# Storing the down factors of a transformer's FFN as one plain fp32 tile instead of a hi and lo pair, and splitting them where they are used

## The chip, the core and the metric

The kernel runs on one core of one Trainium2 chip. The metric is the device time of one execution in microseconds. TensorE (PE in the profile) multiplies matrices, VectorE (DVE) and GpSimd (POOL) do elementwise work, ScalarE (ACT) does activations and copies and also issues the stores spoken of here, and SyncE (SP) issues the loads. PEld is the weight load of TensorE. SBUF is the memory on the core, PSUM the small memory that TensorE writes its products to; DRAM is off the core.

## What is computed

Two transformer blocks over 1024 tokens of width 1024, all in fp32. Each ends in a gated FFN of hidden width 2816, and that is where the change lies:

```python
gu = jnp.einsum('bsd,df->bsf', x, w_gu)
gate, up = gu[..., :FFN_HIDDEN], gu[..., FFN_HIDDEN:]
ffn = jnp.einsum('bsf,fd->bsd', jax.nn.silu(gate) * up, w_down)
...
f = (jax.nn.silu(h @ w_gate[l]) * (h @ w_up[l])) @ w_down[l]
```

## The kernel before

**Three products for one.** TensorE takes fp32r operands, a form of fp32 with a shortened mantissa. To keep fp32's precision the helper `split` (L78) turns an operand into two tiles: `hi` is a copy on ScalarE (L80), `lo` the rest, a subtract on VectorE or GpSimd (L84). `mm3` (L97 to L99) then multiplies hi by hi, hi by lo and lo by hi. So each line of matmuls in the FFN stands three times in a trace.

**Seven products for eight.** Both matrix products of the FFN use a scheme of the Strassen kind. A matrix is cut in 2 x 2 blocks; sums of blocks of the one side (`A11`, `S3`, `S2`, `A22`, `S1`, `A12`, `S4`) meet sums of the other side (`B11`, `T3`, `T2`, `T4`, `T1`, `B21`, `B22`), seven products numbered 1, 7, 6, 4, 5, 2, 3.

**The gate and up stage** (`gate_up`) walks over pairs of 128-wide slices of the hidden width: 11 pairs, the first two of them computed directly. For each later pair it makes the seven products of the gate weights and the seven of the up weights (`product`). A product takes its weight block, or a sum `tt` of two (L925), splits it into a tile `wst` (ACT copy L945, subtract L946 on DVE or POOL), and runs 12 matmuls into a PSUM bank; `after` (L958 to L976) adds the banks up into tiles called `p`, `u` and so on, and `out` (L983 to L994) applies silu and multiplies gate by up. What comes out are the four blocks of the hidden activation, tiles of 128 x 512.

**The store.** `forms` (L1034) is a generator that the loop steps once per product. It makes the sums `S1` to `S4` in place (L1055 to L1064) and calls `store` for each of the seven blocks or sums: 63 calls for nine pairs and 8 plain ones for the last four slices, 71 per FFN. `store` takes a tile `hf`, splits the block into it, and keeps the pair (destination, tile); the DMA is issued by the next call, in `flush`, on ACT's queue (L1023). Tiles `hf` and `wst`, and `ws` of the next stage, come from one ring of six, `slot("w")`: a `wst` can be written only when the tile six places earlier is free, and an `hf` is free only when its store has landed. The blocks themselves live in a ring of twelve, `post`.

**The down stage** (`down`) has five groups, of one slice pair and four times two. A group is the seven products in the order above. For each, 512 KB per slice pair are loaded to a tile `hs` of a ring of seven (the activations' tiles, free by then; in the trace they bear the activations' names, x1B11h and so on), hi and lo side by side; the `down` weights and their sums `st` (L1169) are split into `ws`; 24 matmuls of 128 x 512 follow, and VectorE adds the PSUM banks into accumulators (L1196). `T3`'s sums are POOL's only work there. The last four slices are done directly in `down_last`.

```python
        def store(self, dst, x):

            self.flush()
            t = slot("w", [P, 2, 512], F32R, "hf")
            with soon():
                split(t[:, 0], t[:, 1], x)
            self.stores.append((dst, t.bitcast(F32)))
```

**What sets the order.** The program is compiled by a list scheduler that simulates the engines; `soon()` puts a block ahead of other work that is ready. Each engine runs its instructions strictly in the order that comes out, and so does each queue of DMA issues.

Of the kernel before, what the change touches and what calls it, by code (L numbers as in the profile page):

```python
# [9 lines left out]
F32 = mybir.dt.float32  # L10
F32R = mybir.dt.float32r
# [10 lines left out]
S = 1024  # L22
D = 1024
P = 128
# [14 lines left out]
def two_blocks(ctx: ExitStack, tc: tile.TileContext, a):  # L39
# [16 lines left out]
    def slot(tag, shape, dtype, name):  # L56
        return strm.tile(shape, dtype, tag=tag, bufs=SLOTS[tag], name=name)
# [16 lines left out]
    def soon():  # L74
        return tc.high_priority(offset=4000)
# [132 lines left out]
    for h, l, k0, nk in wu0:  # L208
        for j in range(nk):
            k = k0 + j  # L210
# [566 lines left out]
    class SAct:  # L777
# [4 lines left out]
        def __init__(self, name):  # L782
            self.name = name
            self.high, self.high_done = pool(f"{name}b")
            hi = [self.high.tile([P, 4, 512], F32R, name=f"{name}{n}")
                  for n in ("B11h", "B11l", "B21h", "B21l", "B12l", "B22h", "B22l")]
            self.t = {"B11": hi[0:2], "B21": hi[2:4], "B22": hi[5:7]}

            self.ring, self.n = hi, 0

# [6 lines left out]

        def next(self):
            self.n += 1
            return self.ring[(self.n - 1) % len(self.ring)]  # L800

# [100 lines left out]
    FORMS = ("A11", "S3", "S2", "A22", "S1", "A12", "S4")  # L902
    h_d = [{n: dr.tile([P, 2, 512], F32, name=f"h_d{i}{n}") for n in FORMS} for i in range(NPAIR)]
    hl_d = [dr.tile([P, 2, S], F32, name=f"hl_d{i}") for i in range(NLAST)]

# [90 lines left out]
    class Ffn:  # L996
# [29 lines left out]
        def store(self, dst, x):  # L1026

            self.flush()
            t = slot("w", [P, 2, 512], F32R, "hf")
            with soon():  # L1030
                split(t[:, 0], t[:, 1], x)
            self.stores.append((dst, t.bitcast(F32)))

        def forms(self, i, b):  # L1034


            if i >= NPAIR:
                plain = lambda j, th: self.store(hl_d[2 * (i - NPAIR) + j][:, :, th * 512:(th + 1) * 512], b[j, th])
                for n in ((0, 0), None, (1, 1), (1, 0), None, (0, 1)):
                    if n:  # L1040
                        plain(*n)
                    yield
                return
# [85 lines left out]
        def down(self, wd, res=None):  # L1129
# [24 lines left out]
            for g, np_ in enumerate(SIZES):  # L1154
# [19 lines left out]
                for m, (p, ln, rn) in enumerate(((1, "A11", "B11"), (7, "S3", "T3"), (6, "S2", "T2"), (4, "A22", "T4"),  # L1174
                                                 (5, "S1", "T1"), (2, "A12", "B21"), (3, "S4", "B22"))):
                    hs, ws = act.next(), []
                    for j in range(np_):
                        DMA.dma_start(hs.bitcast(F32)[:, 2 * j:2 * j + 2, :], h_d[f + j][ln])
                        w = slot("w", [P, 2, 512], F32R, "ws")
                        with soon():  # L1180
                            split(w[:, 0], w[:, 1], block(rn, j))
                        ws.append(w)
# [3 lines left out]
                    for c0, n in ((0, 2), (2, 2)) if p in (1, 6, 5, 3) else ((c, 1) for c in range(4)):  # L1186
                        o = a[c0 // 2] if n == 2 else b[c0][:, None, :]
                        for i in range(n):
                            ts = slice((c0 + i) * P, (c0 + i + 1) * P)
                            for j in range(np_):  # L1190
                                mm3(o[:, i, :], hs[:, 2 * j, ts], hs[:, 2 * j + 1, ts], ws[j][:, 0], ws[j][:, 1],
                                    not more and j == 0, j == np_ - 1, more)
# [21 lines left out]
            for n in range(NLAST):  # L1214
                t = act.next()
                DMA.dma_start(flat(t).bitcast(F32), hl_d[n].rearrange("p a b -> p (a b)"))
                self.hs.append(halves(t))
            for n in range(NLAST):
                t = halves(act.next()) if n else [slot("w", [P, S], F32R, "last") for _ in range(2)]
                split(*t, nxt[n])  # L1220
                self.ws.append(t)
# [551 lines left out]
```

## Time and profile before

| | |
|---|---|
| median of 3 runs | 2727.97 us (2725.17 to 2728.15) |
| the profiled execution | 2729.37 us, span on the core 2727.6 us |
| busy | PE 89%, PEld 73%, DVE 67%, ACT 40%, POOL 29% |
| mean granted clock of TensorE | 0.945 |
| DMA | 414.00 MB, mean 152 GB/s |
| gate and up of the first FFN | about 720 to 1227 us |
| down of the first FFN | 1227 to about 1390 us |
| gate and up, down of the second FFN | about 2050 to 2503, 2503 to 2657 us |

A busy PE need not be at its peak: a matmul counts as long as it is in the pipe, at either clock. So the idle time of PE is read stage by stage, with the waits that end it, and the pace of matmuls in a stage without waits serves as measure for the others.

### The profile page before, as it was taken

Reading aid. Unit: us, or ns where it says so; the run is one execution under the profiler, and the core shown is the slowest. Engines: PE = TensorE matmul, PEld = TensorE weight load, DVE = VectorE, ACT = ScalarE, POOL = GpSimd, SP = SyncE. Lnnn points to the kernel's source line nnn. Section 1 sums busy time; section 2 is a strip of 40 time slices with the busy share of each in tenths; the row PEclk is TensorE's granted clock in tenths of the full one; section 3 lists DMA queues with packets and bytes.
Section 4 is the critical chain, followed back from the end, with each engine's and each line's share of the span. In section 5 each row is a group of like instructions: output and inputs, shape, how many; then the busy total and the mean of one; then the engine's idle time right before and its main releaser. Section 6 shows DMA issues by size and latency. Waiting matters only on the chain.

```text
span 2727.6 us, 32854 instructions
## 1 busy us (share of the span) xinstructions
PE 2419.6 (89%) x11584; PEld 1977.9 (73%) x11584; DVE 1840.7 (67%) x3042; ACT 1099.3 (40%) x2013; POOL 784.8 (29%) x751
## 2 busy tenths in 40 slices
PE   8889997998988887889997989898888898999998
PEld 8868775886766665668876868677666666777886
DVE  4889789457667777758776366767555656556775
ACT  4559864243233222323226344445733323334221
POOL 2510235037422122120026042527552212122004
PEclk9999997999998998999998999999989999899999
DMA  4153546333435554567732434553414323337763
GB/s 175 59 153 113 147 137 178 83 98 105 162 127 190 178 179 158 179 249 252 261 141 108 129 105 132 175 159 100 164 58 151 139 108 125 114 124 254 252 226 124
DMA packets 171724, 414.00 MB, mean 152 GB/s; under 512 B 21788, under 2 KB 67868, under 8 KB 170536
## 3 DMA queue, kind: packets, MB, share of 16 engines
q1 hardware_dynamic: 149064, 337.45, 38.2%
q10 hardware_dynamic: 22496, 74.46, 6.8%
q8 instruction: 92, 1.51, 0.2%
q14 instruction: 72, 0.59, 0.1%
HBM read 278.65 MB, written 133.19 MB: 151 GB/s over the span
## 4 chain that ended last, share of the span: by engine, by line
PE 51%; DVE 10%; DMA 5%; POOL 4%; issue 3%; ACT 3%; SPq 0%; ACTq 0%; DVEq 0%; POOLq 0%
PE plg L97 8%; PE plg L98 7%; PE plg L99 7%; PE pmm L97 6%; PE pmm L98 5%; PE pmm L99 5%; PE ptr L99 2%; PE ptr L97 2%; PE ptr L98 2%; DMA raw_c<-in_w_cond_dram 1%; DVE hf L84 1%; DVE wst L946 1%; DVE tt L925 1%; PE plg L337 1%; DVE mod L1278 1%
## 5 line engine op out<-in xcount | busy, mean ns | idle before, releaser
L946 POOL TENSOR_TENSOR wst<-rw,wst 128x512 fp32r<-128x512 f32 x57 | 90.0, 1578 | 406.6 <-ACT wst L945 323.9
L84 POOL TENSOR_TENSOR wl<-raw,wh 128x1024 fp32r<-128x1024 f32 (+2 forms) x28 | 66.1, 2367 | 306.4 <-ACT wh L80 280.1
L337 PE MATMUL plg<-qk,qk 128*128 128x384 f32 (+4 forms) x480 | 127.3, 383 | 29.0 <-DVE mn L350 15.7
L946 DVE TENSOR_TENSOR wst<-tt,wst 128x512 fp32r<-128x512 f32 x144 | 118.5, 826 | 23.7 <-ACT wst L945 23.6
L945 ACT CAST wst<-tt 128x512 fp32r<-128x512 f32 x144 | 88.6, 618 | 73.4 <-PE plg L99 21.4
L1574 DVE TENSOR_TENSOR_SCAN sab<-sab 128x640 f32<-128x640 f32 (+7 forms) x64 | 99.9, 1566 | 20.7 <-ACT sab L1572 19.9
L278 ACT ACTIVATE junk_a<-xi,cand 128x1024 bf16<-128x1024 f32 (+1 forms) x124 | 109.0, 879 | 12.0 <-DVE cand L267 6.9
L337 PEld LDWEIGHTS plg<-qk,qk 128*128 128x128 f32 x480 | 83.7, 202 | 39.6 <-DVE mn L350 17.7
L1196 DVE TENSOR_TENSOR dacc<-dacc,plg 128x1024 f32<-128x1024 f32 x48 | 58.5, 1220 | 55.8 <-PE plg L99 55.8
L80 ACT CAST ws<-st 128x512 fp32r<-128x512 f32 x72 | 44.9, 628 | 127.2 <-PE plg L99 86.8
L162 PE MATMUL pmm<-wh,xh 128*128 128x256 f32 (+1 forms) x320 | 92.2, 289 | 1.7 <-DVE stgl L399 0.8
L163 PE MATMUL pmm<-wl,xh 128*128 128x256 f32 (+1 forms) x320 | 91.5, 286 | 0.0
L164 PE MATMUL pmm<-wh,xl 128*128 128x256 f32 (+1 forms) x320 | 91.4, 286 | 0.0
L351 ACT ACTIVATE e<-e,mn 128x128 f32<-128x128 f32 (+7 forms) x96 | 74.1, 773 | 35.5 <-DVE mn L350 34.5
L994 POOL TENSOR_TENSOR u<-u,u 128x512 f32<-128x512 f32 x36 | 48.2, 1338 | 139.3 <-DVE u L968 113.5
L80 ACT CAST wh<-raw 128x1024 fp32r<-128x1024 f32 x54 | 56.5, 1048 | 69.0 <-PE pmm L98 29.1
L97 PE MATMUL pmm<-xh,wh 128*128 128x512 f32 x192 | 79.2, 412 | 5.8 <-DVE oB L585 3.2
L692 PE MATMUL pmm<-woh,mixh 128*128 128x512 f32 x192 | 78.9, 411 | 5.1 <-ACT mixh L681 2.7
L98 PE MATMUL pmm<-xl,wh 128*128 128x512 f32 x192 | 77.3, 403 | 0.0
L99 PE MATMUL pmm<-xh,wl 128*128 128x512 f32 x192 | 77.2, 402 | 0.0
L693 PE MATMUL pmm<-wol,mixh 128*128 128x512 f32 x192 | 76.3, 397 | 0.0
L694 PE MATMUL pmm<-woh,mixl 128*128 128x512 f32 x192 | 75.8, 399 | 0.3 <-DVE mixl L84 0.3
(733 smaller groups left out, 8361.1 us busy)
## 6 DMA issues: line engine op xcount, KB each, us to landing
raw_c<-in_w_cond_dram SPq DMA_DIRECT2D x48, 512.0 KB, 4.7
qk<-qkd SPq DMA_DIRECT2D x72, 256.0 KB, 5.7
rw<-in_wgu_dram SPq DMA_DIRECT2D x36, 512.0 KB, 3.5
rw<-in_w_down_dram SPq DMA_DIRECT2D x26, 512.0 KB, 5.2
x_d<-acc SPq DMA_DIRECT2D x24, 512.0 KB, 2.6
qk<-qk2d SPq DMA_DIRECT2D x48, 256.0 KB, 4.6
raw<-in_wqk_dram SPq DMA_DIRECT2D x20, 512.0 KB, 4.1
raw<-in_w_down_dram SPq DMA_DIRECT2D x18, 512.0 KB, 5.2
```

What stands on the lines that cost most here:

```text
L80: A.copy(hi, src)
L84: eng.tensor_tensor(lo, src, hi.bitcast(F32), op=OP.subtract)
L97: T.matmul(out, lh, rh, start=start, stop=False, skip_group_check=more)
L98: T.matmul(out, lh, rl, start=False, stop=False, skip_group_check=more)
L99: T.matmul(out, ll, rh, start=False, stop=stop, skip_group_check=more)
L162: T.matmul(o, at(0, k, tb * P, P), h[:, j, :], start=(k == 0), stop=False)
L163: T.matmul(o, at(0, k, tb * P, P), l[:, j, :], start=False, stop=False)
L164: T.matmul(o, at(1, k, tb * P, P), h[:, j, :], start=False, stop=(k == KT - 1))
L278: A.activation(junk_a[:, :L], xi[self.blks[i]], AF.Sign, bias=c, accum_out=self.cnt[:, i:i + 1])
L337: T.matmul(pl[:, c, :n], q[:, isl], k2[:, c * n:(c + 1) * n], start=(j == 0), stop=last)
L946: (G if p in (2, 4) else V).tensor_tensor(wl, x, wh.bitcast(F32), op=OP.subtract)
L1574: V.tensor_tensor_scan(sa[:, ::-1], sa[:, ::-1], sa[:, ::-1], 1.0, op0=OP.mult, op1=OP.bypass)
```

## The change

`store` no longer splits. It keeps the block's own tile, which goes to DRAM as 128 x 512 fp32, 256 KB instead of 512 KB. In `down` the plain blocks are loaded into four half tiles cut from two of the seven tiles of the ring (`next_raw`), and split from there into the other five (`next`), hi on ACT and lo on POOL for products 1, 2, 4 and 3, on DVE for 7, 6 and 5. The subtract of the `ws` of product 3 moves from DVE to POOL. The last four slices are split before `down_last`, with lo on POOL, and the tiles of their weights are drawn from other places.

```diff
-            self.ring, self.n = hi, 0
+            self.ring, self.n, self.m = hi, 0, 0
...
         def next(self):
+
             self.n += 1
-            return self.ring[(self.n - 1) % len(self.ring)]
+            return self.ring[2 + (self.n - 1) % 5]
+
+        def next_raw(self):
+
+            self.m += 1
+            k = (self.m - 1) % 4
+            return self.ring[k // 2].bitcast(F32)[:, k % 2 * 2:k % 2 * 2 + 2, :]
...
-    h_d = [{n: dr.tile([P, 2, 512], F32, name=f"h_d{i}{n}") for n in FORMS} for i in range(NPAIR)]
-    hl_d = [dr.tile([P, 2, S], F32, name=f"hl_d{i}") for i in range(NLAST)]
+    h_d = [{n: dr.tile([P, 512], F32, name=f"h_d{i}{n}") for n in FORMS} for i in range(NPAIR)]
+    hl_d = [dr.tile([P, S], F32, name=f"hl_d{i}") for i in range(NLAST)]
...
             self.flush()
-            t = slot("w", [P, 2, 512], F32R, "hf")
-            with soon():
-                split(t[:, 0], t[:, 1], x)
-            self.stores.append((dst, t.bitcast(F32)))
+            self.stores.append((dst, x))
...
-                plain = lambda j, th: self.store(hl_d[2 * (i - NPAIR) + j][:, :, th * 512:(th + 1) * 512], b[j, th])
+                plain = lambda j, th: self.store(hl_d[2 * (i - NPAIR) + j][:, th * 512:(th + 1) * 512], b[j, th])
...
-                    hs, ws = act.next(), []
+                    hr = act.next_raw()[:, :np_, :]
                     for j in range(np_):
-                        DMA.dma_start(hs.bitcast(F32)[:, 2 * j:2 * j + 2, :], h_d[f + j][ln])
+                        DMA.dma_start(hr[:, j, :], h_d[f + j][ln])
+                    hs = act.next()
+                    hh, hl = hs[:, 0:np_, :], hs[:, 2:2 + np_, :]
+                    ws = []
+                    with soon():
+                        split(hh, hl, hr, lo_eng="pool" if p in (1, 2, 4, 3) else "dve")
+                    for j in range(np_):
                         w = slot("w", [P, 2, 512], F32R, "ws")
                         with soon():
-                            split(w[:, 0], w[:, 1], block(rn, j))
+                            split(w[:, 0], w[:, 1], block(rn, j), lo_eng="pool" if p == 3 else "dve")
                         ws.append(w)
...
-                                mm3(o[:, i, :], hs[:, 2 * j, ts], hs[:, 2 * j + 1, ts], ws[j][:, 0], ws[j][:, 1],
+                                mm3(o[:, i, :], hh[:, j, ts], hl[:, j, ts], ws[j][:, 0], ws[j][:, 1],
                                     not more and j == 0, j == np_ - 1, more)
...
-                t = act.next()
-                DMA.dma_start(flat(t).bitcast(F32), hl_d[n].rearrange("p a b -> p (a b)"))
-                self.hs.append(halves(t))
+                r = flat(act.next_raw())
+                DMA.dma_start(r, hl_d[n])
+                self.hs.append(halves(act.next()))
+                split(*self.hs[n], r, lo_eng="pool")
             for n in range(NLAST):
-                t = halves(act.next()) if n else [slot("w", [P, S], F32R, "last") for _ in range(2)]
+                t = [slot("w", [P, S], F32R, "last") for _ in range(2)] if n < 2 else halves(act.ring[0] if n == 2 else act.next())
                 split(*t, nxt[n])
```

The change moves instructions, since the scheduler places them anew. Three places matter. In the orders below the names of tiles are those of the text above; line numbers after the change lie 7 to 10 higher (L945 is L952, L1023 is L1030, L1169 is L1173).

First, ScalarE in the gate and up stage of the first FFN, around the first stores of the fifth pair (`h_d4`). Before:

```order
L985 ACTIVATE p_8084<-p_8084 128x512
L80 CAST hf<-s_8132 128x512
L945 CAST wst<-rw 128x512
L945 CAST wst<-tt 128x512
L1023 DMA h_d4A_6142<-hf 128x1024
L985 ACTIVATE u_8111<-u_8111 128x512
L80 CAST hf<-u_8168 128x512
L945 CAST wst<-rw 128x512
L1023 DMA h_d4A_6145<-hf 128x1024
L80 CAST hf<-p_8084 128x512
L945 CAST wst<-tt 128x512
L945 CAST wst<-rw 128x512
```

The same stretch of ScalarE's queue with the change:

```order
L992 ACTIVATE p_8015<-p_8015 128x512
L952 CAST wst<-tt 128x512
L1030 DMA h_d4A_6142<-s_8060 128x512
L952 CAST wst<-rw 128x512
L992 ACTIVATE u_8039<-u_8039 128x512
L952 CAST wst<-tt 128x512
L965 COPY p_8336<-pmm 128x512
L952 CAST wst<-tt 128x512
L1030 DMA h_d4A_6145<-u_8093 128x512
L952 CAST wst<-rw 128x512
L952 CAST wst<-tt 128x512
L1030 DMA h_d4A_6147<-p_8015 128x512
```

The copies `hf` are gone from between the copies `wst`; the issues of the stores stay in ScalarE's queue, and each now waits for the block itself, made by POOL or DVE.

Second, POOL in the down stage of the first FFN, from its last multiply of the stage before. Before, these are all its instructions of the rest of that stage:

```order
L994 TENSOR_TENSOR u_10123<-u_10123,u_10261 128x512
L1169 TENSOR_TENSOR st<-rw 128x512
L1169 TENSOR_TENSOR st<-raw,rw 128x512
L1169 TENSOR_TENSOR st<-raw 128x512
L1169 TENSOR_TENSOR st<-rw 128x512 x2
L1169 TENSOR_TENSOR st<-raw 128x512
```

With the change, one group of two slice pairs out of the middle of that stage:

```order
L1173 TENSOR_TENSOR st<-raw 128x512
L1173 TENSOR_TENSOR st<-rw 128x512
L84 TENSOR_TENSOR x1B12l<-x1B11h,x1B12l 128x1024
L84 TENSOR_TENSOR x1B21h<-x1B11h,x1B21h 128x1024
L84 TENSOR_TENSOR x1B22l<-x1B11l,x1B22l 128x1024
L84 TENSOR_TENSOR ws<-rw,ws 128x512
L84 TENSOR_TENSOR x1B21l<-x1B11h,x1B21l 128x1024
L84 TENSOR_TENSOR ws<-raw,ws 128x512
L1173 TENSOR_TENSOR st<-rw 128x512
```

POOL goes from two subtracts per group to eight, four of them 128 x 1024 wide.

Third, TensorE in the first group of two slice pairs of that stage, in product 7 (`S3` by `T3`; its four banks are two `pmm` and two `ptr`, its two slices have one `ws` each). Before, on the first bank `ptr`:

```order
L97 MATMUL ptr_10601<-ws_10588,x1B11l_6107 128x512
L98 MATMUL ptr_10601<-ws_10588,x1B11l_6107 128x512
L99 MATMUL ptr_10601<-ws_10588,x1B11l_6107 128x512
L97 MATMUL ptr_10601<-ws_10594,x1B11l_6107 128x512
L98 MATMUL ptr_10601<-ws_10594,x1B11l_6107 128x512
L99 MATMUL ptr_10601<-ws_10594,x1B11l_6107 128x512
```

With the change, where `x1B22h` holds the same factor and `plg` is a product of the group before:

```order
L98 MATMUL ptr_10406<-ws_10394,x1B22h_6111 128x512
L99 MATMUL ptr_10406<-ws_10394,x1B22h_6111 128x512
L97 MATMUL ptr_10406<-ws_10399,x1B22h_6111 128x512
L98 MATMUL ptr_10407<-ws_10394,x1B22h_6111 128x512
L99 MATMUL ptr_10407<-ws_10394,x1B22h_6111 128x512
L97 MATMUL ptr_10407<-ws_10399,x1B22h_6111 128x512
L97 MATMUL plg_10181<-ws_10335,x1B21l_6109 128x512
```

On the banks `ptr` the second slice's L98 and L99, which need lo tiles, no longer follow its L97, which needs hi tiles alone, and another product is put between; on `pmm` they stood apart before, too.

## Rows read from the trace of the kernel before

**Rows 1.** Windows, three stages: us, busy (x count) of PE, PEld, DVE, ACT, POOL, PEclk, DMA, GB/s.

```profile
720.00:1227.00 507.00, 424.98 (x1673) 325.44 (x1671) 353.20 (x460) 154.59 (x273) 108.10 (x70) 0.93 0.52 182
1227.00:1390.00 163.00, 162.87 (x691) 131.88 (x692) 125.29 (x170) 43.85 (x69) 8.67 (x6) 0.99 0.68 243
...
2050.00:2503.00 453.00, 402.05 (x1603) 309.75 (x1601) 269.23 (x376) 146.71 (x260) 95.77 (x71) 0.95 0.38 139
```

**Rows 2.** Waits of PE, 720 to 1227 us: releaser, us in total, times, longest.

```profile
PE plg L97 <- ACT wst L945: 14.4, 5, 5.0
PE pmm L97 <- ACT wst L945: 13.5, 4, 6.6
PE plg L97 <- DVE u L966: 11.8, 7, 3.4
PE plg L97 <- DVE u L968: 11.4, 10, 3.7
PE pmm L1295 <- ACT mh L80: 9.5, 5, 4.3
PE plg L99 <- DVE wst L946: 8.2, 7, 1.8
```

**Rows 3.** Waits of PE, 2050 to 2503 us.

```profile
PE pmm L97 <- ACT wst L945: 12.1, 7, 3.1
PE plg L97 <- ACT wst L945: 12.0, 7, 1.7
PE plg L97 <- DVE u L968: 8.1, 10, 0.9
PE plg L99 <- DVE wst L946: 4.7, 7, 0.7
PE plg L97 <- ACT ws L80: 3.6, 1, 3.6
```

**Rows 4.** Timeline around one such wait: start, us, engine, line, [idle before it <- releaser].

```profile
2271.17 0.33 ACTq L1023 DMA_DIRECT2D h_d5S<-hf  x1
2271.54 0.62 ACT L945 CAST wst<-raw 128x512 fp32r<-128x512 f32 x1 [0.58 <-DVE hf L84]
...
2272.21 0.79 PE L97 MATMUL pmm<-x3B11h,wst 128*128 128x512 f32 x1 [3.14 <-ACT wst L945]
```

**Rows 5.** Windows, the 2.8 us behind that wait.

```profile
2272.20:2275.00 2.80, 2.79 (x7) 2.21 (x8) 2.09 (x5) 0.77 (x2) 0.00 (x0) 0.50 0.73 294
```

**Rows 6.** Windows, instructions on the tile hf alone: us, DVE and ACT busy (x count).

```profile
720.00:1227.00 507.00, 49.22 (x71) 43.94 (x71) 0.93 0.52 182
```

**Rows 7.** Chain of waits, 720 to 1227 us, its sum by line.

```profile
by line: PE plg L97 11.2%; PE plg L98 10.2%; PE plg L99 10.1%; PE pmm L97 6.0%; PE pmm L98 5.8%; DMA raw_c<-in_w_cond_dram 5.7%; PE pmm L99 5.7%; issue 4.3%; PE ptr L99 3.3%; PE ptr L97 3.2%; PE ptr L98 3.2%; DVE mod L1278 3.2%; DVE hf L84 
```

**Rows 8.** Windows, one group of two slice pairs in the first down stage.

```profile
1252.00:1290.50 38.50, 38.50 (x167) 31.18 (x166) 30.83 (x42) 8.69 (x14) 2.94 (x2) 1.00 0.67 240
```

**Rows 9.** The page, groups: count, then busy us, mean ns, then idle before.

```profile
L84 POOL TENSOR_TENSOR wl<-raw,wh 128x1024 fp32r<-128x1024 f32 (+2 forms) x28 | 66.1, 2367 | 306.4 <-ACT wh L80 280.1
...
L80 ACT CAST wh<-raw 128x1024 fp32r<-128x1024 f32 x54 | 56.5, 1048 | 69.0 <-PE pmm L98 29.1
```

**Rows 10.** Line L84, 0 to 300 us: ns min/median/max, first and last start, form.

```profile
L84 DVE TENSOR_TENSOR wl<-raw,wh x2: 1226/1226/1227, 35.9 to 37.4; 128x1024 fp32r<-128x1024 f32 x2
```

**Rows 11.** Timeline of POOL and of DVE, 1316 to 1319 us.

```profile
1316.86 1.29 POOL L1169 TENSOR_TENSOR st<-rw 128x512 f32<-128x512 f32 x1 [31.61 <-DMA rw<-in_w_down_dram]
...
1316.93 1.76 DVE L84 TENSOR_TENSOR ws<-raw,ws 128x512 fp32r<-128x512 f32 x1
1318.62 0.68 DVE L84 TENSOR_TENSOR ws<-rw,ws 128x512 fp32r<-128x512 f32 x1
```

**Rows 12.** Line L1196, 1227 to 1390 us: ns min/median/max.

```profile
L1196 DVE TENSOR_TENSOR dacc<-dacc,plg x22: 1208/1221/1221, 1256.3 to 1383.5; 128x1024 f32<-128x1024 f32 x22
```

**Rows 13.** Groups of DVE by shape, 1252 to 1290.5 us.

```profile
L84 DVE TENSOR_TENSOR ws<-st,ws 128x512 fp32r<-128x512 f32 x8 | 6.4, 819 | 0.0
```

**Rows 14.** DMA on the tile hf, whole span.

```profile
DMA to landing us min/median/max: 2.6/2.7/8.5
```

## The prediction, written before the changed kernel was run

> **What bounds the kernel now.** I read the windows by stage first, since a busy share over the whole span mixes stages with different limits. In the first down stage PE is busy 162.87 of 163 us: nothing but TensorE's pace counts there, one matmul of 128 x 512 per 163/691 = 0.236 us. In the gate and up stages it is not so: PE is busy 425 of 507 us and 402 of 453, so 82 + 51 = 133 us are idle [rows 1]. At the pace of down, their 1673 and 1603 matmuls would take 395 and 378 us, and the stages are 112 and 75 us longer than that, 187 in all. So behind each idle microsecond stand 0.41 us more in which PE works, but slowly. The reason can be seen behind one stall: after 3.14 us of idleness the next 2.8 us have a granted clock of 0.50, the 1.2 GHz level, and matmuls follow each other at half the pace [rows 4, 5]. I count each idle microsecond of PE as 1.41 us of time.
>
> Next, who ends PE's waits. In the first gate and up stage 27.9 us end with the hi copy of a `wst` on ACT and 8.2 with its lo half on DVE, 36.1 together; 23.2 us end with VectorE reading a PSUM bank (L966, L968); 9.5 with a step of the conditioning rows that are woven into this stage (L1295) [rows 2]. In the second, 24.1 + 4.7 = 28.8 us are for `wst`, 8.1 for L968, and 3.6 for the first `ws` of down [rows 3]. ACT itself is only 30% busy [rows 1], so its copies are late because they wait. The timeline shows how: the issue of a store stands in ACT's queue until DVE has made the lo half of `hf`; the `wst` copy right behind it starts when it is through, and PE has by then been idle for 3.14 us [rows 4]. Besides, each `hf` holds a place of the ring that `wst` needs until its store has landed, 2.6 to 8.5 us after its issue [rows 14].
>
> **What is removed.** In the first gate and up stage 71 splits, 43.9 us of ACT and 49.2 us of DVE [rows 6], and by the code as many in the second. ACT has room, so its share alone is worth nothing; what counts is the queue and the ring. All six places of the ring now go to `wst`, so a weight can be split up to six products ahead, and the order of ACT shows the copies next to each other. For the second stage I take nine tenths of the 28.8 us: 25.9. The first has the same cause, but DVE is 353 of 507 us busy there, and still would be 304 of a shorter stage; also, 5.7% of its chain of waits are loads of the conditioning rows and 3.2% the steps on them [rows 7], which the change leaves. So I take half of 36.1: 18.0. Of the waits for L966 and L968, those of the second stage are 0.8 us each (8.1 by 10), a round trip over PSUM that stays. In the first stage 17 of them come to 23.2 us, of which 17 x 0.8 = 13.6 are that trip; the other 9.6 are a late DVE, and I let them go with its 49 us. Sum of idle time removed: 25.9 + 18.0 + 9.6 = 53.5, times 1.41: **75 us**. The wait of 3.6 us at the start of down [rows 3] goes too, as the last stores hold no place that `ws` needs; counted for both FFNs, 2 x 3.6 x 1.41 = **10 us**. Gain: 85 us. Its ends: nothing if waits only change their name; and if all waits for `wst`, L966 and L968 went, (36.1 + 28.8 + 23.2 + 8.1) x 1.41 + 10 = 146 us.
>
> **What is added, in down.** Take a group of two slice pairs, 38.5 us, in which PE is full, DVE busy 30.8, ACT 8.7, POOL 2.9 [rows 8]. ACT gets seven copies of 128 x 1024 at 1.05 us [rows 9], 7.3 us: it has the room. DVE gets three subtracts of that width at 1.23 [rows 10], 3.7 us, and loses two of 0.68 [rows 11]: 33.1 us, still under 38.5. POOL gets four wide subtracts at 2.37 [rows 9] and two narrow ones at 1.29 [rows 11], 12.1 us, for 15 of 38.5. Each fits by itself. But POOL and DVE disturb each other: a `ws` subtract that began 0.07 us behind a POOL subtract of 1.29 us took 1.76 instead of 0.68 us, so it stood still for 1.08 of the 1.29 [rows 11]. Adding a PSUM bank into an accumulator was never slowed, 1.22 us at most [rows 12]. What DVE loses to POOL's 12.1 us is not in the trace; it lies between nothing and all of it. Before, eight `ws` subtracts of one group were (0.82 - 0.68) x 8 = 1.1 us late [rows 13] to POOL's 2.9. I take half, 6.0, since the new POOL subtracts start where DVE's `ws` subtracts start, at the end of a product. DVE then has 39.1 us of work for 38.5: 0.6 us too much, in eight such groups 5 us. At the start of each down stage the order of PE puts another product between the hi and lo matmuls of product 7, so lo tiles are late there; I price that with the wait found at this place before, 3.6 us [rows 3], twice: 7. Loss: 12 x 1.41 = **17 us**; ends 0 and, with the whole 12.1 lost, (45.2 - 38.5) x 8 = 54, plus 7, times 1.41: 86.
>
> **The rest** costs nothing. Stores and loads are halved; DMA is 68% busy in down [rows 1] and PE waits for no load there. The number of DMA issues on ACT and SP stays. The ring of `hs` falls from seven products to five of 5.7 us (24 x 0.236), far more than a load and a split need. A block must now outlive its store before `post` can reuse it; what is late then is the next product's first tile, a rival below.
>
> **Sum.** The profiled execution took 2729.4 us, 1.4 more than the median of the runs. 2729.4 - 85 + 17 = 2661.4 there, against the median **2660 us**.
>
> **Rivals.** *POOL chokes DVE in down.* If DVE loses all 12.1 us, a group needs 45.2; and DVE cannot fill each gap, since it waits for PE's results too. If half of the 7.7 us that it idles now remain, a group takes 49.0, 10.5 more: 8 x 10.5 + 7 = 91, times 1.41 = 129 us lost against 85 gained, **2772 us**. It decides from (85/1.41 - 7)/8 = 6.7 us per group on. For it: the 1.08 us of standstill [rows 11] and the place of the new subtracts. Against it: POOL's work is spread over the group and accumulation is not touched [rows 12]. The Trainium skill ("SBUF — State Buffer", section "Who interferes with whom") says that a VectorE instruction with two inputs in SBUF and a GpSimd one that reads SBUF exclude each other for a whole instruction, whichever begins first. The 1.76 and the untouched 1.22 us agree with it; by that rule alone every new subtract of POOL can cost DVE its full length, which is this rival.
>
> *The conditioning rows hold the first stage.* If they, and not `wst`, set its pace, the 18.0 and 9.6 us stay: 25.9 x 1.41 + 10 - 17 = 30 us gained, **2698 us**. For it: the 9.5 us of waits for L1295 [rows 2] and the 5.7% [rows 7].
>
> *The waits move to the post ring.* If blocks held by stores delay the next product as `hf` did, only the 9.6 us go: 14 - 17, **2731 us**, no change. For it: stores that land after up to 8.5 us [rows 14]; against it, twelve places instead of six, most stores land in 2.7 us, and each is half as long.
>
> **How the numbers follow.** Forecast 0.67, conditioning rows 0.15, post ring 0.06, choked DVE 0.12. Some 0.2% (5.5 us) is what a measurement of this kernel can tell from no change. Forecast and conditioning rows are both faster: 0.82; the post ring is the same: 0.06; the choke is slower: 0.12. The forecast's own spread goes from all waits gone with the loss of 17 left (2729.4 - 146 + 17 - 1.4 = 2599) to a third of its gain (28 - 17, 2717); the conditioning rows lie inside. So 2600 to 2716; the other two are left out with 0.18.
>
> **What would show it.** Right: no L80 on `hf`; PE idle in the gate and up stages down from 133 to about 75 us, with waits for `wst` a third of what they were; in down, POOL near 15 and DVE near 39 us per group, PE still full but for about 1 us. Wrong: groups of 42 us or more with PE waiting for lo tiles; waits of ACT or DVE for stores of `h_d` before `p` and `u` tiles; or an unchanged first stage with longer waits for L1295.

## The result, and the profile after

The changed kernel takes 2576.26 us in the median of four runs (2570.38 to 2576.77), the kernel before 2728.06 in four runs beside it: a ratio of 0.9433, 95% interval 0.9407 to 0.9459. 152 us are gone; the forecast was 68 (2660 us, 2600 to 2716). The direction was right, the time lies below the range. The profiled execution took 2576.43 us.

The windows of the changed kernel, in the order gate and up of the first and of the second FFN, down of the first and of the second. Columns as in [rows 1].

```profile
720.00:1127.00 407.00, 391.98 (x1658) 310.53 (x1658) 313.73 (x388) 121.07 (x206) 112.07 (x68) 1.00 0.52 171
1962.00:2330.00 368.00, 363.12 (x1548) 290.86 (x1547) 215.83 (x299) 112.04 (x191) 99.41 (x68) 1.00 0.30 103
1127.00:1304.00 177.00, 171.78 (x724) 137.00 (x723) 161.01 (x179) 72.17 (x102) 77.15 (x39) 0.98 0.45 142
2330.00:2503.00 173.00, 169.14 (x733) 136.95 (x732) 158.91 (x167) 80.22 (x117) 77.28 (x39) 1.00 0.46 143
```

In gate and up PE was idle 82 and 51 us [rows 1]; now it is idle 407 - 391.98 = 15 and 368 - 363.12 = 5. The granted clock of these stages rose from 0.93 and 0.95 to 1.00: with the stalls, the running at the lower level behind them [rows 5] went too. DVE is 314 of 407 us busy in the first stage, a higher share than before, and PE is full all the same. The waits of PE that are left, first stage, with engine, line, releaser, us in total, times and longest:

```profile
PE ptr L99 <- DVE wst L953: 4.0, 2, 2.0
PE pmm L97 <- ACT wst L952: 2.8, 2, 2.1
PE plg L97 <- DVE u L973: 2.2, 2, 1.5
PE pmm L99 <- DVE wst L953: 1.6, 1, 1.6
PE pmm L1306 <- ACT mh L80: 1.0, 1, 1.0
PE ptr L97 <- ACT wst L952: 1.0, 2, 0.7
PE plg L97 <- DVE u L975: 0.9, 1, 0.9
PE plg L97 <- ACT wst L952: 0.7, 1, 0.7
```

The lines are 7 to 11 higher than before (L945 is L952, L966 and L968 are L973 and L975, L1295 is L1306, L1196 is L1206). Set against [rows 2]: ACT's `wst`, 27.9 us, is 2.8 + 1.0 + 0.7 = 4.5 now; the 23.2 us for the PSUM readers L966 and L968 are 3.1; the 9.5 us of the conditioning rows are 1.0. In the second stage hardly anything is left of [rows 3]:

```profile
PE ptr L99 <- DVE wst L953: 2.0, 1, 2.0
PE pmm L97 <- ACT wst L952: 1.9, 4, 0.5
PE ptr L97 <- ACT wst L952: 0.7, 1, 0.7
PE plg L97 <- DVE p L978: 0.3, 1, 0.3
```

What ACT waits for tells more than its busy time does. The kernel before, 720 to 1227 us:

```profile
ACT hf L80 <- POOL u L994: 52.6, 11, 6.6
ACT s L983 <- PE pmm L99: 48.9, 9, 6.9
ACT p L985 <- DVE p L971: 35.5, 7, 5.7
ACT u L985 <- DVE u L976: 32.1, 9, 4.7
ACT hf L80 <- POOL p L994: 22.5, 9, 3.5
ACT hf L80 <- DVE s L992: 22.0, 9, 3.5
```

The changed kernel, 720 to 1140 us:

```profile
ACT wst L952 <- PE plg L99: 98.5, 48, 4.8
ACT p L965 <- PE pmm L99: 21.6, 11, 3.4
ACT wst L952 <- PE ptr L99: 17.4, 9, 4.0
ACT wst L952 <- PE pmm L99: 15.4, 7, 4.5
```

Before, ACT waited for results: 97 us (52.6 + 22.5 + 22.0) for the factors that `hf` copies. Now it waits mostly at a `wst` copy until PE gives a place of the ring back: it is as far ahead as the ring lets it.

I took two figures from the start and end times of the trace, both from the first `wst` matmul of a stage to the first `ws` matmul of down. **Copies ahead**: at each moment, the `wst` hi copies that ACT has finished, less a twelfth of the `wst` matmuls that PE has finished (a product has 12), averaged over the time. **Excess**: the sum of what the starts of neighbouring matmuls lie apart beyond 0.235 us, the last gap, in front of the first `ws` matmul, not counted (it is 4.0 us in both stages before and 0.2 in the changed kernel).

| kernel | us, median | copies ahead, 1st and 2nd | excess, us, 1st and 2nd |
|---|---|---|---|
| before | 2728.1 | 2.7, 2.8 | 114, 74 |
| changed | 2576.3 | 5.0, 5.1 | 22, 9 |
| gate and up alone | 2563.6 | 5.0, 5.1 | 25, 9 |
| copy_held | 2697.3 | 2.9, 2.9 | 89, 51 |
| split_idle | 2721.8 | 3.0, 3.1 | 100, 69 |
| copy_idle | 2682.9 | 2.9, 3.0 | 81, 47 |
| copy_pool | 2709.3 | 3.1, 3.2 | 94, 66 |
| split_late | 2729.3 | 2.7, 2.8 | 115, 77 |
| copy_place | 2570.7 | 5.1, 5.1 | 15, 6 |
| own_places | 2587.2 | 5.0, 5.1 | 52, 8 |
| dummy_place | 2575.7 | 5.0, 5.0 | 19, 6 |

Of the 153.2 us by which the span fell, gate, up and down together gave back 90.1 in the first FFN and 69.5 in the second (from the first direct matmul to the first one of the last stage: 772.9 to 682.8, 722.4 to 652.9); the last stages grew from 50.1 to 53.6 and from 43.0 to 50.0.

### The profile page after: what moved, and what is told of

Read it like the earlier page. It is cut to its first block, busy times and chain, and to the rows that moved or that the text cites. A ratio compares the mean times of both kernels' runs of the same rounds, so it can differ in the third digit from the quotient of the medians.

```text
span 2574.4 us, 32838 instructions
## 1 busy us (share of the span) xinstructions
PE 2365.0 (92%) x11584; PEld 1952.2 (76%) x11584; DVE 1829.2 (71%) x2912; ACT 1090.9 (42%) x1949; POOL 940.7 (37%) x817
## 3 DMA queue, kind: packets, MB, share of 16 engines
q8 instruction: 91, 1.49, 0.3%
## 4 chain that ended last, share of the span: by engine, by line
PE 38%; DVE 9%; POOL 3%; issue 2%; DMA 2%; ACT 2%; SPq 0%; DVEq 0%; POOLq 0%; ACTq 0%
PE plg L97 5%; PE plg L98 5%; PE plg L99 5%; PE pmm L98 4%; PE pmm L97 4%; PE pmm L99 4%; DVE ws L84 1%; PE ptr L98 1%; PE ptr L97 1%; PE ptr L99 1%; DVE acc L1206 1%; DVE st L1173 1%; PE plg L337 1%; DVE sab L1585 1%; PE pmm L692 1%
## 5 line engine op out<-in xcount | busy, mean ns | idle before, releaser
L952 ACT CAST wst<-tt 128x512 fp32r<-128x512 f32 x144 | 89.2, 620 | 209.6 <-PE plg L99 120.9
L84 POOL TENSOR_TENSOR wl<-raw,wh 128x1024 fp32r<-128x1024 f32 (+2 forms) x28 | 66.0, 2362 | 230.8 <-ACT wh L80 204.5
L953 DVE TENSOR_TENSOR wst<-tt,wst 128x512 fp32r<-128x512 f32 x144 | 111.7, 776 | 21.5 <-ACT wst L952 20.5
L952 ACT CAST wst<-rw 128x512 fp32r<-128x512 f32 x86 | 53.2, 619 | 123.8 <-PE plg L99 75.9
L1001 POOL TENSOR_TENSOR u<-u,u 128x512 f32<-128x512 f32 x36 | 59.1, 1643 | 85.3 <-DVE u L983 62.0
L80 ACT CAST wh<-raw 128x1024 fp32r<-128x1024 f32 x54 | 56.4, 1048 | 77.0 <-PE pmm L98 28.2
L97 PE MATMUL pmm<-xh,wh 128*128 128x512 f32 x192 | 78.1, 407 | 7.4 <-DVE oB L585 4.8
L84 DVE TENSOR_TENSOR ws<-st,ws 128x512 fp32r<-128x512 f32 x72 | 77.9, 1100 | 2.5 <-ACT ws L80 2.4
L99 PE MATMUL pmm<-xh,wl 128*128 128x512 f32 x192 | 76.5, 398 | 0.0
L1586 POOL TENSOR_TENSOR sab<-sab 128x127 f32<-128x127 f32 (+7 forms) x32 | 44.1, 1379 | 88.5 <-DVE sab L1585 79.9
L98 PE MATMUL pmm<-xl,wh 128*128 128x512 f32 x192 | 76.4, 398 | 0.0
```

The costliest lines, as they stand in the source:

```text
L80: A.copy(hi, src)
L84: eng.tensor_tensor(lo, src, hi.bitcast(F32), op=OP.subtract)
L97: T.matmul(out, lh, rh, start=start, stop=False, skip_group_check=more)
L98: T.matmul(out, lh, rl, start=False, stop=False, skip_group_check=more)
L99: T.matmul(out, ll, rh, start=False, stop=stop, skip_group_check=more)
L952: A.copy(wh, x)
```

## The experiments

Three theories for gate and up. *Ring*: the places that `hf` takes in the `w` ring keep the `wst` copies from running ahead. *Queues*: what counts is that ACT's and DVE's instructions on the factors stand, waiting, in front of the `wst` copies. *Rows*: the conditioning rows set the first stage's pace; the two full stages above have answered that one. Each ratio is to runs of the kernel before on the run's own chip, whose medians lie between 2727 and 2732 us.

**The two halves apart.** The first edit, to the kernel before:

```
-            t = slot("w", [P, 2, 512], F32R, "hf")
-            with soon():
-                split(t[:, 0], t[:, 1], x)
-            self.stores.append((dst, t.bitcast(F32)))
+            self.stores.append((dst[:, 0], x))
+            self.stores.append((dst[:, 1], x))
```

> Only the gate-up half of the change: the factors go to DRAM without a split, straight from their tiles, each block twice (into the hi half and into the lo half), so the stores keep their bytes; down reads and multiplies as before, so that it computes with the plain block in place of lo, and the output is not the reference's. If the whole gain lies in gate-up (its matmuls started 92 and 65 us nearer to each other's pace in the changed kernel): 2727 - 157 = 2570, from 2560 to 2585, and the excess over the matmul pace in the two gate-up stages falls from 114 and 74 us to under 30 and 15. If part of the gain came from down's smaller loads: over 2600.

Measured: 2563.56 us, ratio 0.9391 (0.9374 to 0.9408), 168 us less than before beside it. The whole gain is in gate and up, and it is not one of bytes: the stores and loads here are as many bytes as before. Down works on the plain block in place of lo, with as many instructions as before.

The second edit, to the changed kernel: `h_d` and `hl_d` are two halves again, `store` is that of before, and the loads read one half:

```
-                        DMA.dma_start(hr[:, j, :], h_d[f + j][ln])
+                        DMA.dma_start(hr[:, j, :], h_d[f + j][ln][:, 0])
```

> Only the down half of the change: gate-up splits and stores hi and lo as before; down and the last stage load only the hi half, as if it were the plain block, and split it as the changed kernel does. Lo is left out of the result. The prediction's own term for down was +17 us with ends 0 and 86, so 2745. The trace of the changed kernel shows the matmul excess grown by 9 and 2 us in down and by 3 and 6 us in the last stage, so 2727 + 20 = 2747, from 2738 to 2756, if these losses belong to the split in down; about 2728 if they come only from gate-up ending in another state (ring places, earlier work).

Measured: 2746.46, ratio 1.0058 (1.0038 to 1.0078), 15 us more than before. The halves add up: -168 + 15 = -153, for -152 together. Its last stages last 53.6 and 50.1 us, as in the changed kernel, so 10.6 of the 15 us lie there and not in the groups. In the changed kernel the groups lose more: the excess of the two down stages is 1.6 and 3.5 us before, 5.2 and 5.6 here, and 10.8 and 5.2 in the changed kernel.

**Which part of the split costs.** To the changed kernel's `store`, which puts `(dst, x)` on its list, each run adds one thing. The first, a copy in a `w` place that is stored:

```
+            t = slot("w", [P, 512], F32, "hf")
+            with soon():
+                A.copy(t, x)
-            self.stores.append((dst, x))
+            self.stores.append((dst, t))
```

> The changed kernel, but each factor is copied by ACT into a place of the six-place w ring and stored from there (plain fp32, half the bytes of before): the place is held until its store lands, as hf's was, and DVE has no lo to make. Theory ring (hf's hold on w places kept the wst copies from running ahead): the waits come back, 2640 to 2730. Theory queues (DVE's subtraction and its place in DVE's order were the cost, ACT has room): 2576 to 2595.

Measured: 2697.32, ratio 0.9875 (0.985 to 0.9901). 121 of the 152 us are lost again, without any work for DVE.

The second has the whole split back, in a `w` place from which nothing is stored:

```
+            t = slot("w", [P, 2, 512], F32R, "hf")
+            with soon():
+                split(t[:, 0], t[:, 1], x)
             self.stores.append((dst, x))
```

> The changed kernel, with the removed work put back but nothing stored from it: a w place, ACT's hi copy and DVE's lo subtraction as before, the store still goes from the factor's own tile, so the w place is free as soon as DVE is done. Theory ring (the hold until the store lands): most of the gain stays, 2576 to 2610. Theory queues (the two operations in ACT's and DVE's in-order queues, some 63 x 1.33 us of work on each stage): half the gain or more is lost, 2650 to 2730.

Measured: 2721.77, ratio 0.9966 (0.9949 to 0.9983). A miss for the ring as I had put it, as a hold until the store lands: nothing lands here, and nearly all is lost. So either the queues, or the place itself. The next run leaves the copy on ACT, at its priority, and takes the place away:

```
+            with soon():
+                A.copy(x, x)
             self.stores.append((dst, x))
```

> The changed kernel, with one thing added: ACT copies each factor onto itself, in hf's old place of its order, before it is stored from there. No ring place is taken. In the trace of the kernel before and of copy_held ACT's instruction on the factor waits for the POOL or DVE product that finishes it (94 us in all in the first stage of before), with the wst copies queued behind it. Theory ACT queue: the loss of copy_held comes back whole without the ring, 2670 to 2710. Theory ring: 2576 to 2600, since 126 copies of 0.63 us fit in ACT's idle time.

Measured: 2570.71, ratio 0.9412 (0.9387 to 0.9436). The gain stays. ACT still waits for factors at these copies, in the first stage (720 to 1118 us):

```profile
ACT wst L952 <- PE plg L99: 86.6, 53, 4.0
...
ACT p L1037 <- POOL p L1001: 16.1, 8, 3.9
ACT u L1037 <- POOL u L1001: 14.8, 7, 4.2
ACT u L1037 <- DVE u L1062: 14.6, 6, 3.5
```

That is 45.5 us of waits in front of `wst` copies, and next to nothing of it reaches PE, since the copies are 5 products ahead. So a copy that waits in ACT's queue does not cost by itself. It does not stand at its old point of that queue, though: beside the kernel with a place, which follows, each copy of a factor has 4.2 more `wst` copies in front of it, in the mean of 142. The counterpart gives the copy a `w` place, from which nothing is read:

```
+            t = slot("w", [P, 512], F32, "hf")
+            with soon():
+                A.copy(t, x)
             self.stores.append((dst, x))
```

> The changed kernel, and ACT copies each factor into a place of the w ring from which nothing is read or stored; the store still goes from the factor's own tile. It differs from the kernel with the copy in place only in that a place of the ring is taken in turn, and from copy_held only in that the place is not held until a store lands. If a place taken in turn by something that waits for its factor is what stops the wst copies: 2680 to 2715. If the hold until the store lands is: 2565 to 2600.

Measured: 2682.90, ratio 0.9842 (0.9821 to 0.9863). The same copy, with and without a place in the ring: 2683 against 2571, 112 us. Holding it until a store lands adds 14 more by the medians (2697 - 2683), on two chips, and the intervals of the two ratios touch; a lo half by DVE adds 39 (2722 - 2683). By ACT's order in the traces, all 142 copies of factors stand between the same `wst` copies here, in copy_held, in split_idle and in the kernel before. In its first stage (720 to 1190 us) ACT and PE wait as they did before:

```profile
ACT s L990 <- PE pmm L99: 50.4, 9, 6.9
ACT hf L1038 <- POOL u L1001: 34.0, 9, 8.1
...
ACT hf L1038 <- POOL p L1001: 20.6, 7, 4.3
...
ACT hf L1038 <- DVE s L999: 19.1, 9, 2.9
```

```profile
PE plg L97 <- ACT wst L952: 16.0, 5, 6.7
PE ptr L99 <- DVE wst L953: 7.8, 5, 2.7
```

**Another engine, another priority.** The copy by POOL instead of ACT (`G.tensor_copy(t, x)` in the kernel of copy_held):

> As copy_held (each factor copied into a place of the w ring, held until its store lands), but POOL copies, not ACT, so that ACT's order holds nothing that waits for a factor. Theory ring: 2640 to 2710, as copy_held's 2697. Theory ACT queue: 2576 to 2610, where the rest is POOL's own order (it makes some of wst's lo) and its sharing with DVE.

Measured: 2709.33, ratio 0.9908 (0.988 to 0.9935): the loss is there whichever engine copies. I had expected ACT's order to be free of the factors. It is not: the store's issue stands in it and waits for POOL's copy, with a `wst` copy behind it:

```profile
849.63 0.33 ACTq L1030 DMA_DIRECT2D h_d3A<-hf  x1
850.05 0.62 ACT L952 CAST wst<-tt 128x512 fp32r<-128x512 f32 x1 [4.50 <-POOL hf L1038]
```

So this run takes the copy out of ACT's queue, but not the wait. And the kernel before, without `with soon():` around the split of `hf`:

> The kernel before, with one edit: hf's split is issued without its high priority, so that the scheduler puts it behind the wst copies that stand ready, not ahead of them. Theory ACT queue: the wait of hf's copy for its factor is then mostly over when ACT comes to it; half or more of gate-up's gain without plain stores, 2600 to 2670. Theory ring: the order of the places stays much the same and they are held longer, 2710 to 2760.

Measured: 2729.27, ratio 0.9993 (0.9982 to 1.0005). No change, and there could be none: in the two traces ACT, DVE, POOL and PE have all their instructions in the same order. The run shows that the priority does not set this order; an order with a later split is not tested by it.

**The split kept, in places of its own.** The kernel before, with

```
-            t = slot("w", [P, 2, 512], F32R, "hf")
+            t = self.pp.tile([P, 2, 512], F32R, tag="hf", bufs=1 if self.name == "f1" else 2, name="hf")
...
-        return self.pp.tile([P, 512], dtype, tag="post", bufs=12, name=nm)
+        return self.pp.tile([P, 512], dtype, tag="post", bufs=10, name=nm)
```

> The kernel before, with hf in places of its own (one in the first stage, two in the second; the post ring has 10 places for 12 to make room), its splits at their old priority in ACT's and DVE's order. Theory ring: the second stage, with two places, loses most of its 73.9 us of excess (under 30) and the first, where a split waits for the last one's store, some of its 114; total 2600 to 2690. Theory ACT queue: both stay, 2710 to 2740, the first even longer.

Measured: 2587.17, ratio 0.9466 (0.9444 to 0.9489). Hi and lo are still made by ACT and DVE, stored in full and held until they land, and 144 us are gone. That is below what either theory had. With two places the second stage has an excess of 8 us, as the changed kernel has (9). In the first, with one, PE's waits (720 to 1152 us) begin so:

```profile
PE ptr L97 <- ACT wst L945: 17.0, 5, 7.7
```

and before `hf`'s own instructions their engines sit idle until an earlier store has landed (the tile's view, same stretch: us, times):

```profile
  DMA h_d0S<-hf: 11.0, 3
...
  DMA h_d2S<-hf: 8.4, 4
  DMA h_d0A<-hf: 8.3, 1
```

With a single place the hold until landing costs: 52 us of excess, where the changed kernel's first stage has 22. Post with 10 places for 12 did no harm that shows.

**Too few places, or a place that waits?** The changed kernel, with a place taken by something that waits for no factor:

```
+            t = slot("w", [P, 512], F32, "hf")
+            with soon():
+                G.memset(t[:, 0:8], 0.0)
             self.stores.append((dst, x))
```

> The changed kernel, and for each factor a place of the w ring is taken in turn and given back after POOL has written 8 of its columns with zeros: nothing in it waits for the factor, so the ring is only shorter for wst (one place in three goes to it). Theory length (the wst copies lack places): near copy_idle's 2683, 2650 to 2700. Theory coupling (a place in turn that waits for a factor, which waits for products that need the wst copies behind it): 2570 to 2600, and wst copies four or five ahead of PE.

Measured: 2575.73, ratio 0.944 (0.942 to 0.9459): no loss, though one place in three is taken by something else, and at the same turns: 139 of the 142 places are written between the same `wst` copies as in the kernel before. So a wait for a factor without a place costs nothing (copy_place), nor does a place without a wait (here); the two together cost 112 us (copy_idle). What costs is a place in turn that waits for a factor. I read it so: the factor needs the products of its unit, and the weights of the next products come behind it in the ring's turn, so the copies cannot get further ahead of PE than that. Whether the place itself holds them at run time, or the order that ACT's queue was given because of it, no run separates: the order moved with the place in each.

**The order of PE goes with it.** In the kernel before, product 4 stands directly behind product 5 in PE's order in 18 of 36 cases, and then waits for DVE to read the bank of product 5: the round trips of 0.8 us in [rows 3]. By the program's order it is 16 to 18 of the 36 in every kernel of the table with about 3 copies ahead, and 2 in every one with 5: other products stand between. I have no run in which the order changes alone, so its share is not separated from that of the copies.

**Down: who makes the lo halves.** The changed kernel, without POOL in the groups:

```
-                        split(hh, hl, hr, lo_eng="pool" if p in (1, 2, 4, 3) else "dve")
+                        split(hh, hl, hr, lo_eng="dve")
...
-                            split(w[:, 0], w[:, 1], block(rn, j), lo_eng="pool" if p == 3 else "dve")
+                            split(w[:, 0], w[:, 1], block(rn, j), lo_eng="dve")
```

> The changed kernel with every lo of the down stage on DVE, none on POOL, except in the last stage. By the prediction's terms DVE's work in a group rises by four 128x1024 subtractions of 1.23 us and two 128x512 of 0.68 us and falls by what POOL cost it (half of 12.1): 38.5 + 6.3 - 5.8 = 39.0 or, with some of the accumulations late, 40.5, where PE needs 38.5; so 2576 + 5 to 20 = 2581 to 2596. If POOL's share cost DVE more than it saved (the rival in which POOL holds DVE up): under 2574. If DVE's lo is late for PE in the order: over 2600.

Measured: 2566.86, ratio 0.9423 (0.9398 to 0.9448); the interval overlaps that of the changed kernel. My sum had 2581 to 2596 and missed; the case in which POOL's share costs DVE more than it saves had under 2574. One group of two slice pairs, first the changed kernel, then this one (columns as in [rows 8]):

```profile
1237.00:1275.50 38.50, 38.49 (x169) 31.24 (x168) 38.50 (x44) 14.65 (x21) 14.32 (x7) 1.00 0.52 170
```

```profile
1227.00:1265.50 38.50, 38.50 (x170) 31.56 (x170) 36.92 (x49) 14.65 (x21) 0.00 (x0) 1.00 0.45 149
```

With POOL at work for 14.3 us DVE is busy all the time; with every lo on DVE it does more and is busy 36.9. Over six windows of this length in each kernel, three per down stage, DVE's mean is 36.4 and 36.2 us. The reason by groups of DVE, 1160 to 1300 us, changed kernel first:

```profile
L84 DVE TENSOR_TENSOR ws<-st,ws 128x512 fp32r<-128x512 f32 x29 | 31.9, 1119 | 0.0
L1206 DVE TENSOR_TENSOR dacc<-dacc,plg 128x1024 f32<-128x1024 f32 x21 | 25.0, 1213 | 7.5 <-PE plg L99 7.5
```

```profile
L1206 DVE TENSOR_TENSOR dacc<-dacc,plg 128x1024 f32<-128x1024 f32 x22 | 26.6, 1226 | 6.0 <-PE plg L99 5.9
L84 DVE TENSOR_TENSOR ws<-st,ws 128x512 fp32r<-128x512 f32 x29 | 20.0, 693 | 0.0
```

The same 29 subtracts take 1119 ns beside POOL and 693 without; the accumulation out of PSUM is the same.

PE is not full in every group. In the six windows of the changed kernel it is busy 34.8 to 38.5 us, and in its worst one, 1198.5 to 1237 us, DVE has no gap for the first 14.5 us, while PE is idle for 3.7 of them:

```profile
1198.50:1213.00 14.50, 10.77 (x35) 7.86 (x34) 14.50 (x15) 2.21 (x5) 5.41 (x2) 0.80 0.34 108
```

```profile
1203.78 2.92 POOL L84 TENSOR_TENSOR x1B22l<-x1B11l,x1B22l 128x1024 fp32r<-128x1024 f32 x1 [2.79 <-ACT x1B22l L80]
...
1204.40 2.85 DVE L1173 TENSOR_TENSOR st<-raw,st 128x512 f32<-128x512 f32 x1
...
1207.17 0.67 DVE L1206 TENSOR_TENSOR acc<-acc,pmm 128x512 f32<-128x512 f32 x1
...
1207.90 0.80 PE L97 MATMUL pmm<-ws,x1B12l 128*128 128x512 f32 x1 [2.40 <-DVE acc L1206]
```

A sum `st` that takes 0.68 us in the median of this stage took 2.85 beside a POOL subtract of 2.92; the accumulation behind it came late, PE stood still for 2.40 us, and the granted clock of this window is 0.80. Without POOL's subtracts the waits for `acc` in this stage fall from 4.2 to 0.9 us, and its excess from 10.8 to 2.3.

**The last stage.** First, its four factors split in gate and up, into tiles of the post ring (two stores each), so that the last stage splits weights only:

```
+                    h, l = self.post("hf", F32R), self.post("lf", F32R)
+                    with soon():
+                        split(h, l, b[j, th])
...
+                    self.stores += [(d[:, 0], h.bitcast(F32)), (d[:, 1], l.bitcast(F32))]
```

> The changed kernel, but the four factors of the last stage are split into hi and lo in gate-up, in tiles of the post ring, and loaded as such, so that the last stage splits only its weights. The last stages of the run with down's half alone lasted 53.6 and 50.1 us against 50.1 and 43.0 before; so 2576 - 10 = 2566, from 2558 to 2572, if the splits of the factors make the last stage late and the post ring bears the eight stores; 2576 or more if not.

Measured: 2588.98, ratio 0.9496 (0.9478 to 0.9513): a miss. The last stages do fall, to 46.4 and 43.7 us, so the factors' splits are what makes them long; but the excess of the two down stages rises from 11 and 5 us to 19 each: the loss only went from the last stage into down. Then the high priority for the splits of the last weights (`with soon():` around `split(*t, nxt[n])`):

> The changed kernel, but the splits of the last stage's weights have the high priority that the other splits have, so that DVE makes them ahead of its sums of the last group (L1213, L1216), for which nothing waits. In the trace of the changed kernel PE waits 4.9 and 3.3 us for the lo of the first such weight. 2576 - 8 = 2568, from 2562 to 2573, if that is what the last stage waits for; 2573 to 2580 if the factors' splits on POOL come as late.

Measured: 2573.56, ratio 0.9437 (0.9418 to 0.9456): no change. As with split_late, the edit left every instruction of ACT, DVE, POOL and PE in the same order, so it tests nothing, and the 2.7 us between these medians are what two takes of one order can differ by. In both kernels the first last stage begins with this wait:

```profile
PE pmm L98 <- DVE last L84: 4.9, 1, 4.9
```

And, on lo_dve, one lo of the weights and two of the factors' four shared out between POOL and DVE:

```
-                split(*self.hs[n], r, lo_eng="pool")
+                split(*self.hs[n], r, lo_eng="pool" if n % 2 else "dve")
...
-                split(*t, nxt[n])
+                split(*t, nxt[n], lo_eng="pool" if n == 1 else "dve")
```

> The changed kernel with every lo of the down stage on DVE; in the last stage POOL makes the lo of the second weight (DVE's came 4.9 us late for PE, behind accumulations of the last group that wait for PE) and of every other factor, DVE the rest. With the second weight's lo out of DVE's order the last stages lose their 4.9 and 3.3 us waits: 2567 - 7 = 2560, from 2554 to 2567. If POOL, which has the next stage's lo to make, is as late: 2567 to 2575.

Measured: 2574.45, ratio 0.9433 (0.9412 to 0.9453): a miss, with last stages of 57.6 and 52.0 us. The wait for the weight's lo is gone there, and PE waits 4.0 and 3.3 us for two of the factors' lo halves by DVE instead. Which order of DVE would give these 10 us back stays open.

**A version below both.** The edits of lo_dve and copy_place together:

> The changed kernel with every lo of the down stage on DVE and with ACT's copy of each factor onto itself. The first was 9 us under the changed kernel and the second 6 us under it, in down and in gate-up apart; if these are no chance of the runs, 2576 - 15 = 2561, from 2554 to 2568; if they are, 2570 to 2578.

Measured: 2560.71, ratio 0.9388 (0.9368 to 0.9407), 15.6 us under the changed kernel's median; the intervals just touch. The copy is work that nothing needs; it moves the scheduler to an order with 6 us less excess in the first stage and 3 in the second. As a design only the other edit is worth keeping.

## Why the prediction was wrong

**The loss, 17 us: right in size by luck.** Down alone measured 15, but 10.6 of them lie in the last stage, at which the sum had nothing; some 4 are left for the groups and their start, which had all 17. That POOL takes much of its time from DVE was borne out: in 1160 to 1300 us each of the 29 `ws<-st` subtracts is 0.43 us longer than without POOL, 12.4 us in all. The work of a group came near what was worked out (DVE 39.1 forecast, a mean of 36.4 in windows of 38.5 us; POOL 15, and 13.3 to 17.8). The choked-DVE rival (2772) had its mechanism and not its price: PE does wait for a DVE that POOL holds up, but not in each group, and the excess of the two down stages grew by 9 and 2 us, where the rival had 129.

**The gain, 85 us: mis-sized; 168 measured.** The factor 1.41 came near: 133 - 20 = 113 us of idleness went in the changed kernel, 1.49 us of the 168 for each. It was the idle time removed that I had at 53.5 + 7.2 = 61, with these steps wrong:
- "*A round trip over PSUM that stays*", 21.7 us, the largest named one. It went: 23.2 + 8.1 us became 3.1 + 0, so 28.2 us left where I had 9.6. What changed with it is PE's order: where the product whose bank is needed stood directly behind in 18 of 36 cases, it does in 2.
- "*So I take half of 36.1*", as DVE and the conditioning rows would hold the first stage. They held nothing: `wst` waits fell from 36.1 to 10.1 us (4.5 for hi, 4.0 + 1.6 for lo), 26 for my 18, with DVE busy 314 of 407 us. The rival of the conditioning rows (2698) falls with it; their own 9.5 us of PE waits, for which I had nothing, are 1.0 now.
- The waits outside the two lists, which the upper end of 146 us leaves out too: of the 113 us some 19 belong to none of these rows.

The second stage's `wst` (25.9 forecast, 28.8 to 4.6 us) and the 7.2 us at the start of down came out as forecast.

**The mechanism, half right.** The ring was named, but with two reasons that the runs turn down as the main ones: the hold "until its store has landed" is worth 14 us at most (copy_held against copy_idle), and an instruction on ACT that waits for the factor, as `hf` does in [rows 4], costs nothing that shows once the copies are ahead (copy_place). What counted is that something which waits for a result took its turn in the ring of the operands that PE needs to make results. The waits did not move to the post ring (2731): twelve places, or ten, bear the stores.

## What to carry to other kernels

Give tiles that wait for a result a ring of their own, apart from the ring whose tiles let the engine run ahead: one shared turn cost 112 us here, a ring of two places in its stead nothing that shows. Before a run without an effect is read, look whether its order differs at all: two edits of a priority here left it as it was. When a bottleneck engine waits in many small ways, look first at how far its feeder is ahead; if that can rise, waits of other names (PSUM trips, side work) go too, and should be counted with it. Before work is given to POOL to relieve DVE, look at what DVE's subtracts take beside POOL: here, sharing gained nothing. A term that comes out right in sum can still lie in another stage.

## What the runs showed of the hardware

POOL's subtracts slow DVE's by about what they relieve it of. Over both down stages of the changed kernel (190 and 184 us) POOL is busy 82.94 and 82.57 us and DVE 173.94 and 169.87; with no lo on POOL they are 28.13 and 26.75, and DVE 171.52 and 164.21 (181 and 183 us), with more work done:

```profile
sum 374.00, PE 364.93 PEld 293.62 DVE 343.81 ACT 160.75 POOL 165.52; mean PE 182.46 PEld 146.81 DVE 171.90 ACT 80.38 POOL 82.76
```

```profile
sum 364.00, PE 360.86 PEld 291.37 DVE 335.74 ACT 161.87 POOL 54.87; mean PE 180.43 PEld 145.68 DVE 167.87 ACT 80.94 POOL 27.44
```

So 110.65 us less of POOL left DVE 8.07 us less busy, though DVE took the subtracts over. The Trainium skill ("SBUF — State Buffer", section "Who interferes with whom") has a VectorE instruction with two inputs in SBUF contend with a GpSimd instruction that reads SBUF, under an exclusive lock; the 1119 against 693 ns agree, and the unchanged 1213 and 1226 ns of the accumulation out of PSUM agree as well.
